# One decoder block on one Trainium2 core: the expert gather by moving residual rows and transposing, its first batch in a written TensorE order, and another order of the last gate sums and the final normalisation

## The chip, the cores and the metric

The kernel runs on one core of one Trainium2 chip, as one program. Its engines work from queues of their own and meet through semaphores: TensorE (PE: matmuls from SBUF into PSUM; PEld are its weight loads), VectorE (DVE), ScalarE (ACT), GpSimd (POOL) and SyncE (SP), which here issues nearly all DMAs. In a matmul one operand is loaded as weights and is called stationary, the other streams through and is called moving. The metric is the device time of an execution in microseconds, shown as the median of several; less is better.

## The reference

One hybrid decoder block on 256 tokens of width 2048, all fp32:

```
xn = rms_norm(x, g_mix);  z = xn @ w_in                       # 7168 columns
o  = [ HGRN2 heads (gated linear recurrence) , gated short convolution ]
x  = x + o @ w_out
hn = rms_norm(x, g_ffn)
group = top1(softmax(hn @ w_router_group))                    # 4 groups
e1,e2 = top2(softmax(logits of the 8 experts of that group))  # 32 experts
x  = x + sum over e1,e2 of  weight_e * (silu(hn@w_gate[e]) * (hn@w_up[e])) @ w_down[e]
ple = rms_norm(p @ w_ple, g_ple)
x  = x + sigmoid(x @ w_ple_gate) * ple
out = rms_norm(x, g_final)
```

All 32 experts' weights are read: 3 x 4 MB an expert.

## The kernel before

The tokens are two tiles of 128 (index j in the code); x1[j] holds the residual rows of tile j, tokens on the partitions, 2048 columns.

Weights. A list of pieces, nearly all of 1 MB, is laid down in the order of use: input projection, output projection, gate and up weights of the experts in eight batches of four, then down weights and the embedding gate's weights. `give` issues the next piece into a free slot, `take` hands out the oldest one, `refill_slot` gives a slot back and issues the next piece into it (or, while `want` is above zero, keeps the slot for another tile: three slots during the first batch, three in batch 3). A piece is thus issued once the slot's last reader is done, in the order of the list, from SP's queue.

Experts. After the routing, R1 holds for each token and expert the place of the token among that expert's 32 places. For batch b, `slot_perm` builds from it a 0/1 matrix of tokens by 4 x 32 places, scaled by the token's normalisation factor (tile Pg, lines 781 and 791). `gather(b)` returns the gathered, transposed tokens xg (16 groups of 128 columns by 128 places) and a function for a quarter of it. A quarter is eight 128x128 matmuls whose stationary operand is every fourth column of 512 of x1[j] and whose moving operand is the 0/1 matrix (line 797); VectorE multiplies the result by the gain (line 800):

```
MM(ps[:, kk], x1[j][:, kq * 512 + kk:(kq + 1) * 512:4], Pr[j], start=kk == 0 and j == 0, stop=kk == 3 and j == 1)
```

`product(b, ...)` (line 856) then makes gk and uk, 64 matmuls each in four quarters: a quarter takes four pieces, one for each expert of the batch, and each matmul writes the 32 PSUM partitions of its expert, four experts side by side. A slot is given back after its last matmul of the quarter. `hidden` makes silu(gk)·uk and transposes it (line 869). In the first batch the quarters of the gather are called between the quarters of gk; for the later ones the whole `gather(b + 1)` is called between gk and uk of batch b. `embed` (lines 881, 901) prepares the embedding beside batch 4 and 5, `weights_w` (lines 806 to 831) the routing weights beside the first product.

Down products. The first four batches are done at full width (lines 1050, 1039), the last four in five column chunks (lines 1177, 1161), each followed by the embedding gate of the chunk before: `residual` adds the chunk to x1 and transposes it (lines 1084 to 1096), `gate_mm` multiplies it with the split weights (lines 1118 to 1120) into the sums G. For the last chunk `gate_sum` puts the sum so far into a PSUM bank by a matmul with the identity (line 1128) and the gate's matmuls add to it. Eight such groups (two tiles by four times 512 columns) end the kernel: `gate` takes sigmoid and multiplies by ple, `update` adds to x1 and squares (line 1221), `mean_square`, `token_scale` and `store` are the final normalisation (lines 1234, 1235).

Order. The code is recorded and a scheduler orders each engine's instructions by priority and readiness under its own costs; `tc.issue_after(i)` forces what is recorded in it behind instruction i, and `seq()` uses it with TensorE's last instruction in state["pe"], so that a stretch of TensorE's order is the order of the code. PSUM tiles come from two pools of four banks, `bank` and `misc`; `tmp4` tiles rotate over three buffers.

Of the kernel before, what the change touches and what calls it, by code (L numbers as in the profile page):

```python
# [11 lines left out]
AF = mybir.ActivationFunctionType  # L12
OP = mybir.AluOpType
# [22 lines left out]
def kernel(ctx, tc, a, out, dbg=None):  # L36
# [24 lines left out]
    def misc(shape=(P, 512), name="ms"):  # L61
        return psB.tile(list(shape), F32, tag="ms", name=nm(name))
# [716 lines left out]
    def slot_perm(Pm, b, j):  # L779

        V.tensor_tensor(Pm[:, j], R1[:, j, 4 * b:4 * b + 4].unsqueeze(2).to_broadcast([P, 4, CAP]),
                        iota1.unsqueeze(1).to_broadcast([P, 4, CAP]), OP.is_equal)

    def gather(b):

        xg = slot(xg_slots[b % 2], [P, KT, P], name="xg")
        Pm = tmp4([P, 2, 4, CAP], "Pg")
        Pr = [Pm[:, j].rearrange("p e c -> p (e c)") for j in range(2)]
        for j in range(2):
            slot_perm(Pm, b, j)  # L790
            V.tensor_scalar(Pr[j], Pr[j], r1[:, j:j + 1], None, OP.mult)  # L791

        def quarter(kq):
            ps = misc((P, 4, P), "xg")
            for j in range(2):
                for kk in range(4):
                    MM(ps[:, kk], x1[j][:, kq * 512 + kk:(kq + 1) * 512:4], Pr[j], start=kk == 0 and j == 0,  # L797
                       stop=kk == 3 and j == 1)
            ks = slice(4 * kq, 4 * kq + 4)
            state["xg"] = V.tensor_tensor(xg[:, ks], ps, gfq[:, kq].unsqueeze(2).to_broadcast([P, 4, P]), OP.mult)  # L800
        return xg, quarter

# [43 lines left out]
    def product(b, xg, name, before=None):  # L846
        bk = bank(name=name)
        for kp in range(4):
            if before is not None:
                before(kp)  # L850
            four = [take() for _ in range(4)]
            for kk in range(4):
                k = 4 * kp + kk
                for e in range(4):
                    q = slice(32 * e, 32 * e + 32)
                    MM(bk[q], xg[:, k, q], four[e][1][:, kk], start=k == 0, stop=k == KT - 1)  # L856
            for e in range(4):
                refill_slot(four[e][0])
            step()
        return bk  # L860
# [60 lines left out]
    xg_slots = [8, None]  # L921
    xg, quarter = gather(0)

    quarter(0)
    first_xg = state["xg"]

    def first_quarters(kp):
        if kp > 0:
            quarter(kp)

    for b in range(NB):
# [18 lines left out]
        if b + 1 < NB:  # L950
            xn, quarter = gather(b + 1)
            for kq in range(4):
                quarter(kq)
        uk = product(b, xg, "uk")
# [112 lines left out]

    def seq():

        return tc.issue_after(state["pe"].ins) if "pe" in state else ExitStack()  # L1070

# [78 lines left out]

    job = None
    for ci, (c0, w) in enumerate(CHUNKS):
        last = ci == len(CHUNKS) - 1
# [12 lines left out]
        for b in range(NBR, NB):  # L1166
# [31 lines left out]
            if last and b >= NB - 2:  # L1198
                if b == NB - 2:
                    parts = {}  # L1200
                    for n in range(3):
                        gate_sum(0, n, bank)
                n = 2 * (b - NB + 2)
                for q in range(n, n + 2):
                    parts[q] = split_gate(q, [own[q // 2]], free)
        combine(*late)
        if not last:
            job = embedding_gate(c0, w, acc, ci == 0)


    xT = residual(c0, w, acc)
    with tc.issue_after(state["x2T"].ins):
        gate_sum(0, 3, misc)
        gate_sum(1, 0, misc)
    ssf = st("ssf", (2, 4))
# [10 lines left out]

    def token_scale(j):
        rsqrt_cols(rf[:, j:j + 1], msf[:, j:j + 1], 1, "rft")

    def store(j):  # L1230
        for n in range(4):
            ns = slice(n * 512, (n + 1) * 512)
            g = Gs[j][:, ns]
            V.scalar_tensor_tensor(g, x1[j][:, ns], rf[:, j:j + 1], gfin[:, ns], OP.mult, OP.mult)  # L1234
            nc.sync.dma_start(out[0, j * P:(j + 1) * P, ns], g)

    def gate(j, n):
        if (j, n) not in gb:
            with tc.issue_after(state["gate"].ins):
                gate_sum(j, n, misc)  # L1240
        gate_mm(gb[j, n], xT, parts[n], j, False)
        ns = slice(n * 512, (n + 1) * 512)
        g = Gs[j][:, ns]
        state["sig"] = A.activation(g, gb[j, n], AF.Sigmoid)
        V.tensor_tensor(g, g, ple[j][:, ns], OP.mult)

    def update(j, n):
        ns = slice(n * 512, (n + 1) * 512)
        g = Gs[j][:, ns]
        V.tensor_tensor(x1[j][:, ns], g, x1[j][:, ns], OP.add)  # L1250
        square(j, n)

    for n in range(4):
        gate(0, n)
        update(0, n)
    for n in range(4):
        gate(1, n)
        if n == 1:
            mean_square(0)
    with tc.issue_after(state["sig"].ins):  # L1260
        A.activation(warm, epsc, AF.Sqrt)
        update(1, 0)
        token_scale(0)
        update(1, 1)
        update(1, 2)
        update(1, 3)
        store(0)
        mean_square(1)
        token_scale(1)
        store(1)  # L1270

# [42 lines left out]
```

## Time and profile before

| what | value |
|---|---|
| median of 3 runs | 1502.43 us (1502.09 to 1502.65) |
| the profiled execution | 1500.68 us, span 1499.0 us |
| TensorE busy | 1333.2 us, 89% of the span |
| TensorE weight loads | 811.9 us, 54% |
| VectorE, ScalarE, GpSimd busy | 466.1, 341.1, 21.9 us |
| DMA | 505.62 MB, 337 GB/s on average |
| gate, up and down weights | 128 pieces each, 1024.0 KB a piece |
| mean granted TensorE clock | 0.965 of 2.4 GHz |

The profile is one execution on the chip. A record of TensorE is one pass: an fp32 matmul leaves two records, a transpose one. The time of a record includes the tail in which the next one already runs, so a run of records is read from start to start. The DMA share is the mean busy share of the 16 DMA engines and passes 1.0 a little where they are full. The name on the left of an arrow is what an instruction writes; a bracket at the end of a row is the idle time before it and what ended it.

### The profile page before, as it was taken

To read this page: it belongs to the slowest core of one execution; us is meant where nothing else is said; L and a number is where in the kernel's file an instruction comes from. 1 tells how busy PE (TensorE), PEld (TensorE's weight loads), DVE (VectorE), ACT (ScalarE), POOL (GpSimd) and SP (SyncE) were. 2 spreads that over 40 slices of the span, in tenths; PEclk is the share of its full clock that TensorE was granted. 3 is DMA by queue.
4 is the path that set the end of the run, shared out by engine and by line. 5 is a ranking of instruction groups with operands and counts; after the bars stand their busy time and mean duration, and the time that the engine had idled before them with its cause. 6 is when DMAs were issued, how large, how long until landed. Compare 5 with 4: busy or idle time off the path is not lost. (4 is left out here: it accounts for less than half of the span.)

```text
span 1499.0 us, 19727 instructions
## 1 busy us (share of the span) xinstructions
PE 1333.2 (89%) x8490; PEld 811.9 (54%) x8490; DVE 466.1 (31%) x750; ACT 341.1 (23%) x469; POOL 21.9 (1%) x36
## 2 busy tenths in 40 slices
PE   9999999999999986869698787866689999898995
PEld 9998999999897642415152333311122222253663
DVE  6778756575543100001011221100001111213455
ACT  6666455354441000000001000000010000222233
POOL 1001100000000000000000000000000000000000
PEclk9999999999999999989999998988999999999998
DMA  8855625479546999999999999999999999999991
GB/s 308 267 163 182 214 97 197 157 250 339 209 163 267 402 421 422 421 421 420 421 421 422 421 378 422 420 421 422 421 420 422 421 420 388 392 390 391 366 336 57
DMA packets 140377, 505.62 MB, mean 337 GB/s; under 512 B 12361, under 2 KB 33210, under 8 KB 98814
## 3 DMA queue, kind: packets, MB, share of 16 engines
q1 hardware_dynamic: 139726, 501.74, 85.9%
q0 software_dynamic: 384, 2.36, 0.4%
q8 instruction: 68, 1.11, 0.3%
q10 hardware_dynamic: 176, 0.22, 0.1%
q14 instruction: 23, 0.19, 0.0%
HBM read 502.19 MB, written 2.10 MB: 336 GB/s over the span
## 5 line engine op out<-in xcount | busy, mean ns | idle before, releaser
L856 PE MATMUL uk<-w,xg 128*32 128x512 f32 x1024 | 197.1, 687 | 92.8 <-DMA w<-in_w_up_dram 92.8
L337 PE MATMUL mm<-xh,whl 128*128 128x256 f32 x768 | 218.8, 285 | 0.3 <-ACT xh L259 0.3
L339 PE MATMUL mm<-xh,whl 128*128 128x256 f32 x768 | 217.6, 283 | 0.1
L338 PE MATMUL mm<-xl,whl 128*128 128x256 f32 x768 | 217.3, 283 | 0.3 <-DVE xl L260 0.2
L301 DVE TENSOR_TENSOR whl<-w,whl 128x1024 fp32r<-128x1024 f32 (+1 forms) x146 | 175.8, 1212 | 109.9 <-ACT whl L300 109.6
L300 ACT CAST whl<-w 128x1024 fp32r<-128x1024 f32 (+1 forms) x146 | 150.5, 1036 | 187.4 <-PE mm L339 112.1
L856 PE MATMUL gk<-w,xg 128*32 128x512 f32 x1024 | 165.7, 640 | 23.4 <-DMA w<-in_w_gate_dram 23.4
L856 PEld LDWEIGHTS uk<-w,xg 128*32 128x32 f32 x1024 | 43.3, 122 | 240.4 <-DMA w<-in_w_up_dram 165.9
L338 PEld LDWEIGHTS mm<-xl,whl 128*128 128x128 f32 x768 | 147.3, 192 | 0.9 <-DVE xl L260 0.8
L337 PEld LDWEIGHTS mm<-xh,whl 128*128 128x128 f32 x768 | 147.1, 192 | 1.1 <-ACT xh L259 0.5
L339 PEld LDWEIGHTS mm<-xh,whl 128*128 128x128 f32 x768 | 147.2, 192 | 0.4 <-DVE whl L301 0.3
L1050 PE MATMUL y<-w,hT 128*32 128x512 f32 x512 | 134.6, 603 | 6.5 <-PEq L1019 6.5
L797 PEld LDWEIGHTS xg<-Pg,x 128*128 128x128 f32 x512 | 121.4, 328 | 16.6 <-issue 15.4
L865 DVE TENSOR_TENSOR sg<-sg,uk 128x512 f32<-128x512 f32 x8 | 5.5, 688 | 389.1 <-PE uk L856 389.1
L797 PE MATMUL xg<-Pg,x 128*128 128x128 f32 x512 | 125.4, 401 | 0.7 <-DVE Pg L791 0.7
L856 PEld LDWEIGHTS gk<-w,xg 128*32 128x32 f32 x1024 | 38.6, 116 | 123.0 <-issue 73.7
L1050 PEld LDWEIGHTS y<-w,hT 128*32 128x32 f32 x512 | 37.9, 111 | 100.9 <-issue 96.9
L1177 PE MATMUL y<-w,hT 128*32 128x512 f32 (+1 forms) x640 | 77.0, 534 | 15.0 <-DMA w<-in_w_down_dram 15.0
L870 ACT COPY hT<-hT 128x256 f32<-128x256 f32 x8 | 3.0, 372 | 301.9 <-PE hT L869 301.9
L1040 DVE TENSOR_TENSOR x<-acc,x 128x512 f32<-128x512 f32 x32 | 22.1, 692 | 138.0 <-PE acc L1039 138.0
L800 DVE TENSOR_TENSOR xg<-xg,gfq 128x512 f32<-128x512 f32 x32 | 22.1, 692 | 126.3 <-PE xg L797 126.3
L1177 PEld LDWEIGHTS y<-w,hT 128*32 128x32 f32 x640 | 21.3, 112 | 64.2 <-issue 30.5
(293 smaller groups left out, 1340.2 us busy)
## 6 DMA issues: line engine op xcount, KB each, us to landing
w<-in_w_gate_dram SPq DMA_DIRECT2D x128, 1024.0 KB, 19.8
w<-in_w_up_dram SPq DMA_DIRECT2D x128, 1024.0 KB, 19.8
w<-in_w_down_dram SPq DMA_DIRECT2D x128, 1024.0 KB, 16.5
w<-in_w_in_dram SPq DMA_DIRECT2D x55, 1024.0 KB, 5.3
w<-in_w_out_dram SPq DMA_DIRECT2D x16, 1024.0 KB, 6.7
w<-in_w_ple_gate_dram SPq DMA_DIRECT2D x16, 1024.0 KB, 12.6
xa<-in_x_dram SPq DMA_DIRECT2D x8, 256.0 KB, 4.8
x<-in_x_dram POOLq DMA_DIRECT2D x2, 1024.0 KB, 8.1
```

Source lines behind the costliest of these rows:

```text
L300: state["copy"] = A.copy(wh, wf)
L301: V.tensor_tensor(wl, wf, f32(wh), OP.subtract)
L337: MM(o, wh[:, kk, cs], b_h, start=first, stop=False)
L338: MM(o, wh[:, kk, cs], b_l, start=False, stop=False)
L339: MM(o, wl[:, kk, cs], b_h, start=False, stop=last)
L797: MM(ps[:, kk], x1[j][:, kq * 512 + kk:(kq + 1) * 512:4], Pr[j], start=kk == 0 and j == 0, stop=kk == 3 and j == 1)
L800: state["xg"] = V.tensor_tensor(xg[:, ks], ps, gfq[:, kq].unsqueeze(2).to_broadcast([P, 4, P]), OP.mult)
L856: MM(bk[q], xg[:, k, q], four[e][1][:, kk], start=k == 0, stop=k == KT - 1)
L865: V.tensor_tensor(sg, sg, uk, OP.mult)
L1040: V.tensor_tensor(x1[j][:, ns], acc, x1[j][:, ns], OP.add)
L1050: MM(ys[n][q], hT[k // 2][:, k % 2, b, q], four[e][1][:, n * 512:(n + 1) * 512], start=k == 0, stop=k == 3)
L1177: last_y = MM(ys[q, :w], hT[f // 2][:, f % 2, b, q], held[e][1][:, f], start=f == 0, stop=f == 3)
```

## The change

The gather is done in two steps. `rows(kq, j)` multiplies with the 0/1 matrix as the stationary operand and 512 columns of x1[j] as the moving one, both tiles into one PSUM bank; ScalarE copies the gathered rows to SBUF. `turn(kq)` transposes every fourth column of them, four transposes a quarter, and VectorE multiplies by the gain as before. In the first batch these calls are put in TensorE's order by `seq`, the steps of the next quarters ahead of each product quarter. In the last chunk three gate sums stay where they were, one more is recorded before the last accumulation, one before `residual` and two behind it, so that one of eight is left among the groups. The squares come right behind the residual add of their group, and the two final scale chains are mixed with the output products.

```
+    def seq():
+
+        return tc.issue_after(state["pe"].ins) if "pe" in state else ExitStack()
...
-        def quarter(kq):
+        gts, pss = [], []
+
+        def rows(kq, j):
+
+            if j == 0:
+                pss.append(misc(name="xr"))
+            state["pe"] = MM(pss[kq], Pr[j], x1[j][:, kq * 512:(kq + 1) * 512], start=j == 0, stop=j == 1)
+            if j == 1:
+                if kq % 2 == 0:
+                    gts.append(tmp4([P, 2, 512], "gt"))
+                A.copy(gts[-1][:, kq % 2], pss[kq])
+
+        def turn(kq):
+
             ps = misc((P, 4, P), "xg")
-            for j in range(2):
-                for kk in range(4):
-                    MM(ps[:, kk], x1[j][:, kq * 512 + kk:(kq + 1) * 512:4], Pr[j], start=kk == 0 and j == 0,
-                       stop=kk == 3 and j == 1)
+            for kk in range(4):
+                state["pe"] = nc.tensor.transpose(ps[:, kk], gts[kq // 2][:, kq % 2, kk::4], ident)
             ks = slice(4 * kq, 4 * kq + 4)
             state["xg"] = V.tensor_tensor(xg[:, ks], ps, gfq[:, kq].unsqueeze(2).to_broadcast([P, 4, P]), OP.mult)
-        return xg, quarter
+        return xg, rows, turn
...
+            with seq() if before is not None else ExitStack():
+                for kk in range(4):
...
-    xg, quarter = gather(0)
-
-    quarter(0)
+    xg, rows, turn = gather(0)
+
+    def first(*steps):
+        for f, *args in steps:
+            with seq():
+                f(*args)
+
+    rows(0, 0)
+    first((rows, 0, 1), (rows, 1, 0), (turn, 0), (rows, 1, 1))
     first_xg = state["xg"]
 
     def first_quarters(kp):
         if kp > 0:
-            quarter(kp)
+            first((turn, kp))
+        if 0 < kp < 3:
+            first((rows, kp + 1, 0), (rows, kp + 1, 1))
...
-            xn, quarter = gather(b + 1)
+            xn, rows, turn = gather(b + 1)
             for kq in range(4):
-                quarter(kq)
+                rows(kq, 0)
+                rows(kq, 1)
+                turn(kq)
...
             if last and b >= NB - 2:
-                if b == NB - 2:
-                    parts = {}
-                    for n in range(3):
-                        gate_sum(0, n, bank)
                 n = 2 * (b - NB + 2)
                 for q in range(n, n + 2):
                     parts[q] = split_gate(q, [own[q // 2]], free)
+                if b == NB - 2:
+                    for n in range(3):
+                        gate_sum(0, n, bank)
+                else:
+                    gate_sum(0, 3, misc)
...
+    gate_sum(1, 0, misc)
     xT = residual(c0, w, acc)
-    with tc.issue_after(state["x2T"].ins):
-        gate_sum(0, 3, misc)
-        gate_sum(1, 0, misc)
+    gate_sum(1, 1, bank)
+    gate_sum(1, 2, misc)
...
     for n in range(4):
         gate(0, n)
-        update(0, n)
+    mean_square(0)
     for n in range(4):
         gate(1, n)
-        if n == 1:
-            mean_square(0)
     with tc.issue_after(state["sig"].ins):
-        A.activation(warm, epsc, AF.Sqrt)
-        update(1, 0)
-        token_scale(0)
-        update(1, 1)
-        update(1, 2)
-        update(1, 3)
-        store(0)
-        mean_square(1)
-        token_scale(1)
-        store(1)
+        rsqrt_cols(rf[:, 0:1], msf[:, 0:1], 1, "rft")
+    store(0, 0)
+    store(0, 1)
+    mean_square(1)
+    with tc.issue_after(state["sig"].ins):
+        rsqrt_cols(rf[:, 1:2], msf[:, 1:2], 1, "rft")
+    store(0, 2)
+    store(0, 3)
+    for n in range(4):
+        store(1, n)
```

**The first batch.** TensorE from the last routing instruction (cntT) to the second quarter of gk, before; xg is the gathered tile or its PSUM bank, x_327 and x_328 are x1[0] and x1[1], gk's other matmuls are left out:

```order
L768 MATMUL cntT_4942<-consts,cnt_4940 1x128
L797 MATMUL xg_4969<-Pg_4964,x_327_4098 128x128 x4
L797 MATMUL xg_4969<-Pg_4964,x_328_4100 128x128 x4
L797 MATMUL xg_4998<-Pg_4964,x_327_4098 128x128 x4
L856 MATMUL gk_4979<-w_4210,xg_4963 32x512
...
L797 MATMUL xg_4998<-Pg_4964,x_328_4100 128x128 x4
L797 MATMUL xg_5032<-Pg_4964,x_327_4098 128x128 x4
L856 MATMUL gk_4979<-w_4338,xg_4963 32x512
```

The same stretch of TensorE after; xr are the gathered rows in PSUM, gt their copy in SBUF:

```order
L768 MATMUL cntT_4942<-consts,cnt_4940 1x128
L803 MATMUL xr_4969<-x_327_4098,Pg_4964 128x512
L803 MATMUL xr_4969<-x_328_4100,Pg_4964 128x512
L803 MATMUL xr_4974<-x_327_4098,Pg_4964 128x512
L813 MATMUL xg_4976<-consts,gt_4972 128x128 x4
L803 MATMUL xr_4974<-x_328_4100,Pg_4964 128x512
L872 MATMUL gk_4984<-w_4210,xg_4963 32x512
...
L813 MATMUL xg_5003<-consts,gt_4972 128x128 x4
L803 MATMUL xr_5009<-x_327_4098,Pg_4964 128x512
L803 MATMUL xr_5009<-x_328_4100,Pg_4964 128x512
L872 MATMUL gk_4984<-w_4338,xg_4963 32x512
```

Ahead of each product quarter 12 or 8 gather matmuls of 128 columns have become row matmuls of 512 columns and four transposes, with the rows of the next quarter ahead of the product.

ScalarE at the same place before, from the table load of the square root (L179) to the routing weights (eg, ee):

```order
L179 ACT_TABLE_LOAD
L179 ACTIVATE r1t_4893<-ms_428_4889 128x2
L812 ACT_TABLE_LOAD
L812 ACTIVATE eg_5100<-eg_5100,r_429_4890 128x4
L813 ACTIVATE ee_5102<-ee_5102,r_429_4890 128x8
```

And after:

```order
L179 ACT_TABLE_LOAD
L179 ACTIVATE r1t_4893<-ms_428_4889 128x2
L807 COPY gt_4972<-xr_4969 128x512
L807 COPY gt_4972<-xr_4974 128x512
L827 ACT_TABLE_LOAD
L827 ACTIVATE eg_5102<-eg_5102,r_429_4890 128x4
L828 ACTIVATE ee_5104<-ee_5104,r_429_4890 128x8
```

The two copies of gathered rows now stand between the square root and the exponential's table load.

**Batch 5.** TensorE between the first and the second quarter of gk, where gb is a row broadcast of `embed`, before:

```order
L856 MATMUL gk_6319<-w_6263,xg_6129 32x512
L797 MATMUL xg_6479<-Pg_6464,x_327_4098 128x128 x3
L797 MATMUL xg_6479<-Pg_6464,x_328_4100 128x128 x4
L797 MATMUL xg_6489<-Pg_6464,x_327_4098 128x128 x3
L856 MATMUL gk_6319<-w_6265,xg_6129 32x512
L797 MATMUL xg_6489<-Pg_6464,x_327_4098 128x128
L797 MATMUL xg_6489<-Pg_6464,x_328_4100 128x128 x4
L797 MATMUL xg_6499<-Pg_6464,x_327_4098 128x128 x4
L797 MATMUL xg_6499<-Pg_6464,x_328_4100 128x128 x4
L881 MATMUL gb_6539<-dg_6534,consts 128x512
L856 MATMUL gk_6319<-w_6267,xg_6129 32x512
L881 MATMUL gb_6572<-dg_6567,consts 128x512
```

And after, where the main run of the second quarter begins with the last row:

```order
L803 MATMUL xr_6492<-x_327_4098,Pg_6476 128x512
L803 MATMUL xr_6492<-x_328_4100,Pg_6476 128x512
L872 MATMUL gk_6331<-w_6277,xg_6139 32x512
L813 MATMUL xg_6496<-consts,gt_6484 128x128 x4
L803 MATMUL xr_6502<-x_327_4098,Pg_6476 128x512
L803 MATMUL xr_6502<-x_328_4100,Pg_6476 128x512
L872 MATMUL gk_6331<-w_6279,xg_6139 32x512
L813 MATMUL xg_6507<-consts,gt_6505 128x128 x4
L803 MATMUL xr_6513<-x_327_4098,Pg_6476 128x512
L803 MATMUL xr_6513<-x_328_4100,Pg_6476 128x512
L813 MATMUL xg_6517<-consts,gt_6505 128x128 x2
L872 MATMUL gk_6331<-w_6281,xg_6139 32x512
```

The gather stands between the same products as before, and the two broadcasts that stood ahead of the second quarter's main run are behind it.

**The last chunk.** TensorE from the last two accumulations (acc) to the first matmul of the first group (Gf), before:

```order
L1161 MATMUL acc_8910<-y_9042,PwT_6128 128x256 x2
L1161 MATMUL acc_8910<-y_9091,PwT_6128 128x256 x2
L1092 MATMUL x2T_9106<-consts,x_327_4098 128x128
L1092 MATMUL x2T_9106<-consts,x_328_4100 128x128
...
L1128 MATMUL Gf_9113<-G_7976,consts 128x512
L1128 MATMUL Gf_9115<-G_7977,consts 128x512
L1118 MATMUL Gf_9062<-ghl_9068,x2T_9105 128x512
```

And after:

```order
L1187 MATMUL acc_8926<-y_9058,PwT_6138 128x256 x2
L1153 MATMUL Gf_9117<-G_7992,consts 128x512
L1187 MATMUL acc_8926<-y_9107,PwT_6138 128x256 x2
L1153 MATMUL Gf_9121<-G_7993,consts 128x512
L1117 MATMUL x2T_9126<-consts,x_327_4098 128x128
L1117 MATMUL x2T_9126<-consts,x_328_4100 128x128
...
L1153 MATMUL Gf_9133<-G_7993,consts 128x512
L1153 MATMUL Gf_9135<-G_7993,consts 128x512
L1143 MATMUL Gf_9084<-ghl_9078,x2T_9125 128x512
```

Two gate sums now stand ahead of the transposes, two others behind them; of the three that stood among the groups one is left.

ScalarE over the last groups before, sigmoids (L1244) and squares (L1221, junk):

```order
L1244 ACTIVATE G_7977<-Gf_9184 128x512
L1244 ACTIVATE G_7977<-Gf_9194 128x512
L1261 ACT_TABLE_LOAD
L1261 ACTIVATE warm<-epsc 128x1
L1221 ACTIVATE junk_9206,ssf_9117<-x_328_4100 128x512
L179 ACTIVATE rft_9208<-msf_9119 128x1
```

And after:

```order
L1268 ACTIVATE G_7993<-Gf_9135 128x512
L1248 ACTIVATE junk_9206,ssf_9137<-x_328_4100 128x512
L1248 ACTIVATE junk_9217,ssf_9137<-x_328_4100 128x512
L1268 ACTIVATE G_7993<-Gf_9219 128x512
L179 ACT_TABLE_LOAD
L179 ACTIVATE rft_9232<-msf_9139 128x1
L1248 ACTIVATE junk_9230,ssf_9137<-x_328_4100 128x512
```

Three squares of the second token tile stand ahead of the last sigmoid, where none stood.

## Rows read from the trace of the kernel before

**Rows 1.** Windows (us): PE, PEld, DVE, ACT, POOL busy (count), clock, DMA share, GB/s

```profile
466.00:482.00 16.00, 16.00 (x102) 10.49 (x102) 3.80 (x22) 2.25 (x5) 0.00 (x0) 1.00 0.26 83
482.00:510.00 28.00, 28.00 (x164) 21.08 (x167) 4.89 (x10) 0.60 (x1) 0.00 (x0) 1.00 1.01 422
510.00:514.00 4.00, 4.00 (x40) 1.17 (x36) 0.00 (x0) 0.00 (x0) 0.00 (x0) 1.00 0.66 219
514.00:870.00 356.00, 287.68 (x1506) 126.66 (x1498) 32.24 (x83) 10.33 (x19) 1.08 (x2) 0.94 1.01 421
870.00:882.00 12.00, 12.00 (x60) 4.59 (x63) 7.29 (x20) 0.93 (x2) 0.00 (x0) 1.00 0.72 283
...
1101.00:1240.00 139.00, 139.00 (x496) 41.17 (x495) 16.61 (x24) 8.21 (x15) 0.00 (x0) 1.00 1.01 420
```

**Rows 2.** Timeline of SP's DMA issues: start, length, engine, line, out<-in, count

```profile
479.86 16.91 SPq L162 DMA_DIRECT2D w<-in_w_up_dram  x11
...
858.05 0.86 SPq L162 DMA_DIRECT2D w<-in_w_gate_dram  x2
877.81 2.92 SPq L162 DMA_DIRECT2D w<-in_w_up_dram  x3
```

**Rows 3.** Timeline of TensorE, first batch

```profile
462.94 5.84 PE L797 MATMUL xg<-Pg,x 128*128 128x128 f32 x24
...
468.70 3.64 PE L856 MATMUL gk<-w,xg 128*32 128x512 f32 x32
472.28 4.00 PE L797 MATMUL xg<-Pg,x 128*128 128x128 f32 x16
476.20 3.64 PE L856 MATMUL gk<-w,xg 128*32 128x512 f32 x32
```

**Rows 4.** Timeline of TensorE, batch 5

```profile
851.12 3.30 PE L797 MATMUL xg<-Pg,x 128*128 128x128 f32 x14
...
859.03 1.04 PE L856 MATMUL gk<-w,xg 128*32 128x512 f32 x2
...
875.00 3.62 PE L856 MATMUL gk<-w,xg 128*32 128x512 f32 x26
```

**Rows 5.** The chain that ended last: start, length, what

```profile
1252.03 7.08 PE acc L1039 x16
...
1297.01 1.02 PE x2T L1092 x8
...
1465.61 1.94 PE acc L1161 x8
...
1468.05 0.33 PE x2T L1092
...
1468.93 1.72 PE Gf L1128 x4
...
1488.12 2.74 DVE G L1234 x4
```

**Rows 6.** Timeline of TensorE: the transposes of a hidden tile

```profile
522.94 0.75 PE L869 MATMUL hT<-consts,sg 128*128 128x128 f32 x4
```

**Rows 7.** ScalarE's groups: busy us, mean ns, idle before

```profile
L1058 ACT COPY y<-y 128x512 f32<-128x512 f32 x16 | 8.6, 592 | 138.4 <-PE y L1050 137.9
```

**Rows 8.** Timeline of ScalarE, first batch

```profile
456.55 0.20 ACT L179 ACTIVATE r1t<-ms 128x2 f32<-128x2 f32 x1
456.77 1.28 ACT L812 ACT_TABLE_LOAD   x1
467.74 0.30 ACT L812 ACTIVATE eg<-eg,r 128x4 f32<-128x4 f32 x1 [9.69 <-DVE eg L806]
```

**Rows 9.** Timeline of VectorE: the routing weights; the last output products

```profile
470.26 0.17 DVE L829 TENSOR_TENSOR ee<-ee,gp 128x16 f32<-128x16 f32 x1
...
1492.36 2.74 DVE L1234 SCALAR_TENSOR_TENSOR G<-x,rf,gfin 128x512 f32<-128x512 f32 x4
```

**Rows 10.** Timeline of TensorE at the lower clock

```profile
898.67 1.92 PE L856 MATMUL uk<-w,xg 128*32 128x512 f32 x2 [1.44 <-DMA w<-in_w_up_dram]
```

More of the change, by code (lines that the diff above doesn't have):

```diff
@@ L851, in product @@
             four = [take() for _ in range(4)]
[L852 to L856, printed above, removed]
+            with seq() if before is not None else ExitStack():
+                for kk in range(4):
+                    k = 4 * kp + kk
+                    for e in range(4):
+                        q = slice(32 * e, 32 * e + 32)
+                        last = MM(bk[q], xg[:, k, q], four[e][1][:, kk], start=k == 0, stop=k == KT - 1)
+            state["pe"] = last
             for e in range(4):
@@ L1066 @@
     gate_slots = []
-    def seq():
-        return tc.issue_after(state["pe"].ins) if "pe" in state else ExitStack()
+    state.pop("pe")
     def accumulator(w):
@@ L1151 @@
     job = None
+    parts = {}
     for ci, (c0, w) in enumerate(CHUNKS):
@@ L1225, in mean_square, with store @@
         V.tensor_scalar(msf[:, j:j + 1], msf[:, j:j + 1], 1.0 / D, EPS, OP.mult, OP.add)
[L1227 to L1235, printed above, removed]
+    def store(j, n):
+        ns = slice(n * 512, (n + 1) * 512)
+        g = Gs[j][:, ns]
+        V.scalar_tensor_tensor(g, x1[j][:, ns], rf[:, j:j + 1], gfin[:, ns], OP.mult, OP.mult)
+        nc.sync.dma_start(out[0, j * P:(j + 1) * P, ns], g)
     def gate(j, n):
         if (j, n) not in gb:
-            with tc.issue_after(state["gate"].ins):
-                gate_sum(j, n, misc)
-        gate_mm(gb[j, n], xT, parts[n], j, False)
+            gate_sum(j, n, misc)
+        with seq():
+            gate_mm(gb[j, n], xT, parts[n], j, False)
+        state["pe"] = state["gate"]
         ns = slice(n * 512, (n + 1) * 512)
@@ L1245, in gate @@
         V.tensor_tensor(g, g, ple[j][:, ns], OP.mult)
-    def update(j, n):
-        ns = slice(n * 512, (n + 1) * 512)
-        g = Gs[j][:, ns]
         V.tensor_tensor(x1[j][:, ns], g, x1[j][:, ns], OP.add)
```

## The prediction

> **What bounds the kernel now.** I read the windows first, then the SP queue, then TensorE around each hole, then the chain at the end. The windows [rows 1] show a data-bound kernel: from 514 to 870 us the DMA engines stand at share 1.01 and 421 GB/s while TensorE is busy 287.68 of 356 us. The reader should look for the three stretches that fall below that rate: 466 to 482 us at 83 GB/s, 510 to 514 at 219, 870 to 882 at 283. Against 421 GB/s they lose 16·(1−83/421) = 12.8, 4·(1−219/421) = 1.92 and 12·(1−283/421) = 3.93 us. What is lost there is not caught up: behind each hole the engines run at their ceiling again, and at 1101 to 1240 us TensorE (139.00 of 139.00 us) and the DMA engines (420 GB/s) are full together. That later part starts when the last gate and up weights arrive and holds nothing that is tied to absolute time, so I pass an earlier stream to the end one for one.
>
> The SP queue tells what makes the holes [rows 2]. The run of refills begins at 479.86 us; in the later hole nothing is issued between 858.05 (plus 0.86) and 877.81. A slot is free when its last product of a quarter is done, so the holes are TensorE being late. TensorE there [rows 3, 4]: in the first batch 24 records of gather from 462.94 us, a product quarter from 468.70, 16 gather records of 4.00 us from 472.28, the next quarter from 476.20, whose first freed slot gives the issue at 479.86 (3.66 later). In batch 5 the gather sits between two quarters of the product, the second of which starts its main run only at 875.00.
>
> **The gather.** A quarter of a gather costs 4.00 us now (an fp32 matmul leaves two records, a batch 64). After, it is two matmuls of 512 columns and four transposes. The trace has the first shape under another name: 16 records in 7.08 us [rows 5], 0.44 each, so the two take 4·0.44 = 1.77 us. Transposes with every fourth column as the stationary operand exist too, one record each: four are begun at 522.94 and end 0.75 later [rows 6]. Four unstrided ones take 1.02/2 = 0.51 us [rows 5]; four at the pace of today's gather records would take 1.0. I take 0.58, near the strided row without its tail. So 2.35 us a quarter (2.3 to 2.8) against 4.00. New is a ScalarE copy between the two steps, 592 ns as such copies take now [rows 7]; with some 0.25 us of drain and signalling (an estimate from the 0.16 that a 0.75 us group outlasts its pace, and the hand-over) it is 0.85 us that other TensorE work must cover.
>
> *First batch.* Rows of quarter 0: 462.94 to 464.71. The copy ends about 465.55; under it runs the first half of quarter 1's rows. Transposes to 466.2, VectorE's scaling to about 467.0, under it the second half of quarter 1. The first product starts at 467.0 instead of 468.70. Then 3.58 of product (468.70 to 472.28), 0.58 of transposes and 1.77 of rows: the second quarter starts at 472.9 instead of 476.20, and the first big refill is issued 3.3 us earlier, near 476.55. Later refills come every 5.9 us for four pieces of 1024 KB, which take 10 us to move at 421 GB/s, so the stream then holds. The cover that could go: VectorE's scaling of quarter 1 stands behind the routing weights. Now ScalarE loads the exponential's table at 456.77, long before its use at 467.74 [rows 8]; after, the two copies stand ahead of that load. Second copy done at 467.8, load 1.28, exponentials from 469.1, 1.35 us later than now; the weights, now done at 470.26+0.17 [rows 9], end at 471.8, the scaling at 472.5, still 0.4 us ahead of the product at 472.9. A further 1.28 us there, the price of one more load, would leave 0.9 uncovered: 2.4 as the lower end.
>
> In rows 8 the load stands right behind the square root (456.55 plus 0.20, then 456.77) and takes 1.28 us. The Trainium skill, page "ScalarE: Activation LUTs", section "What ACT_TABLE_LOAD costs", puts a drain of about 1380 ns beside a load of about 1283 ns, some 2.66 us a switch. The trace agrees with its load and shows no drain. By the row this place gives 3.3 us; by the rule 1.38 more stands in the chain, 1.0 of it in the open, and the place gives 2.3.
>
> *Second hole.* It comes because the whole gather for batch 1 runs before the first up quarter frees a slot. After, four pieces are refilled after each of the next three gate quarters (476.5, 482.5, 488): 12 pieces, 30 us, from about 478.5 to 508. The first up quarter has 8.5 of gather, about 1 of uncovered copies and up to 4.8 of product in front and frees its slots near 502. The hole closes: 1.9 (0 to 1.9).
>
> *Third hole.* TensorE now does 14 gather records from 851.12, the first quarter's main run, then the rest of the gather among single products (1.04 each [rows 4]) and two row broadcasts, then the second run at 875.00. After: 1.77 of rows in place of 3.30, so the first run, now over some 1.1 us before 859.03, ends near 856.4; then three and a half sets of transposes and three of rows, 3.5·0.58+3·1.77 = 7.3, three singles 3.0, one copy in the open 0.85; the broadcasts move behind. The second run starts near 867.6, not 875.00, the issue comes near 870.4, not 877.81. Data follows an issue by about 2 us (479.86 to 482), so of the 12·283/421 = 8.1 us' worth moved between 870 and 882 only about 2 came from the late issue, and the older pieces last to about 876 at the full rate. The hole closes with 3 us in hand: 3.9 (0 to 3.9; not below, since the new quarter at its upper 2.8 and the open copy stay under 4.00). In the other batches TensorE waits for data anyway, and 6.6 us less work there is worth nothing.
>
> **The end.** From the last down product on TensorE has one gap [rows 5]: the two last accumulations end at 1465.61+1.94 = 1467.55, the transposes start at 1468.05 and, with a wait between them for the second VectorE add, end at 1468.93. After, one gate sum stands between the accumulations and one behind them: the 0.5 us are filled, and the four transposes run in 0.51 instead of 0.88. The eight groups and eight sums stay as many and as long; two sums still cover the split of the transposed tile (1.72). TensorE is done 0.9 us earlier. Behind it two effects meet. ScalarE has the square of the group before last ahead of the last sigmoid; it waits for VectorE, which has a multiply and an add for each group and no slack, so the last sigmoid starts up to 0.85 us later than TensorE allows. On the other side the second scale chain, which now puts 1492.36−(1488.12+2.74) = 1.5 us between the two runs of output products [rows 5, 9], is mixed into the first run and costs about 0.5. I take them as equal: 0.9 for the end (−0.5 to 1.5).
>
> **Sum.** 3.3+1.9+3.9+0.9 = 10.0 us. The profiled execution took 1500.68 us (span 1499.0), so 1490.7 for it; the median shown, 1502.43, lies 1.75 higher, and for a median I forecast 1492.4. The bounds: 2.4+0+0−0.5 = 1.9 to 3.5+1.9+3.9+1.5 = 10.8 us less, 1500.5 to 1491.6.
>
> **Rivals.**
> *The third hole stays.* With less to do TensorE waits more for data, and its clock may fall. It is granted 0.94 in 514 to 870 us [rows 1], and one pair of product records takes 1.92 us at 898.67 [rows 10] against 1.04. At that level the 11 us of gather and singles double and the issue slips past 877. Against it: 1.00 in 870 to 882. Gain 6.1, 1496.3 us. The Trainium skill, page "TensorE: Matmul & The Clock Gate", section "HAM oscillation — how this bites in real kernels", says that a TensorE with too little work between its waits for data keeps falling back to the half clock; the 0.94 agrees in kind, and by that rule this rival is what comes.
> *The weights come late.* One more load's worth in ScalarE's part of the first batch: 0.9 us less, 1493.3.
> *Hidden after all.* If something behind the holes made up for lost time, only the end would count: 1501.5. Against it: share 1.01 from 514 to 870.
> *Slower: the first batch loses the clock.* The new order makes TensorE wait for a copy and a scaling before the first product. If the clock fell to its lower level there (1.2 in place of 2.4 GHz, records twice as long, as in rows 10), the first product would last 7.2 us, the second quarter start at 478.7 and its first refill be issued near 486, 6 us later than now, which eats what the other three places give (6.7). If it lasts into the third quarter, each further quarter (11.9 us for 10 us of data) and the up quarter with its gather (some 27 us) open new holes, the largest of 17 us: from the third quarter on it decides for slower; through the up quarter 6+2+17−6.7 = 18 us more, about 1520. Against it: 1.00 in 466 to 514 us.
>
> **How the numbers follow.** Forecast (all four places, 1491.3 to 1493.0): 0.62. Third hole stays, wholly or half: 0.15. Weights late: 0.08. Hidden: 0.06. Slower: 0.04. More than forecast: 0.05. This kernel's runs tell about 0.2% (3 us) from no change. Faster by that are 0.62+0.15+0.08+0.05 = 0.90, less 0.02 for small mishaps that add up: 0.88; within 0.06+0.02 = 0.08; slower 0.04. The range 1490.6 to 1497.0 holds the forecast, the late weights, the open third hole and a little more than the forecast.
>
> **What would show it.** Right: the run of refills begins near 476.5 us; no window below 415 GB/s between 480 and 1090; everything behind starts about 9 us earlier; 2.35 us of TensorE for a quarter of the gather; no TensorE gap from the last accumulation to the last gate matmul. Wrong: a hole that remains near 870; a first product over 4 us; four transposes near 1 us; a second quarter that waits for VectorE's scaling; a tail behind the last matmul over 1 us longer than now.

## The result and the profile after

The changed kernel takes 1492.12 us (median of four, 1491.95 to 1492.46) against 1502.54 for the kernel before in the same set (1502.09 to 1505.28): ratio 0.9927, 95% interval 0.991 to 0.9944. 10.4 us are gone; the forecast was 10.0, 1492.4 us. The profiled execution took 1492.06 us (span 1490.4), 8.6 us less than the profiled one of before, which lay 1.8 below its median.

The windows of the changed kernel, to be laid beside [rows 1]:

```profile
466.00:482.00 16.00, 16.00 (x115) 5.30 (x114) 5.05 (x26) 3.91 (x8) 0.00 (x0) 1.00 0.46 171
510.00:514.00 4.00, 3.09 (x26) 1.26 (x19) 0.78 (x2) 0.37 (x1) 0.00 (x0) 1.00 1.01 422
514.00:870.00 356.00, 279.88 (x1306) 77.41 (x1305) 34.62 (x88) 21.66 (x38) 1.07 (x2) 0.92 1.01 421
870.00:882.00 12.00, 10.38 (x73) 2.77 (x72) 5.43 (x17) 2.25 (x3) 0.00 (x0) 1.00 1.02 424
```

The last column, the rate of the stream in GB/s, is to be read first. The first stretch went from 83 to 171 GB/s and now loses 16·(1−171/421) = 9.5 us where it lost 12.8; the second and third holes are gone. At 882 us the stream is 3.3+1.9+3.9 = 9.1 us ahead. SP's issues give the same two dates [rows 2]:

```profile
476.53 2.04 SPq L162 DMA_DIRECT2D w<-in_w_up_dram  x4
...
865.86 14.18 SPq L162 DMA_DIRECT2D w<-in_w_up_dram  x10
```

The run of refills begins at 476.53 instead of 479.86, and the issue that came at 877.81 comes at 865.86. TensorE in the first batch, beside [rows 3]:

```profile
462.69 2.81 PE L803 MATMUL xr<-x,Pg 128*128 128x512 f32 x6
465.37 0.75 PE L813 MATMUL xg<-consts,gt 128*128 128x128 f32 x4
465.96 1.02 PE L803 MATMUL xr<-x,Pg 128*128 128x512 f32 x2
466.91 3.64 PE L872 MATMUL gk<-w,xg 128*32 128x512 f32 x32
470.48 0.75 PE L813 MATMUL xg<-consts,gt 128*128 128x128 f32 x4
471.07 1.88 PE L803 MATMUL xr<-x,Pg 128*128 128x512 f32 x4
472.88 3.64 PE L872 MATMUL gk<-w,xg 128*32 128x512 f32 x32
```

Four transposes step on after 0.59 us, four records of rows after 1.81: 2.40 us a quarter (forecast 2.35, before 4.00). The product quarters start at 466.91 and 472.88 (forecast 467.0 and 472.9). No row has an idle time in brackets: copy and scaling are covered. The routing weights, which could have spoilt that, on ScalarE and VectorE, beside [rows 8, 9]:

```profile
467.02 0.59 ACT L807 COPY gt<-xr 128x512 f32<-128x512 f32 x1 [1.70 <-PE xr L803]
467.62 1.28 ACT L827 ACT_TABLE_LOAD   x1
468.92 0.30 ACT L827 ACTIVATE eg<-eg,r 128x4 f32<-128x4 f32 x1
```
```profile
471.34 0.17 DVE L844 TENSOR_TENSOR ee<-ee,gp 128x16 f32<-128x16 f32 x1
471.43 0.68 DVE L815 TENSOR_TENSOR xg<-xg,gfq 128x512 f32<-128x512 f32 x1
```

The load starts 0.01 us after the copy's end and takes 1.28; weights done at 471.5 (forecast 471.8), scaling at 472.11, 0.77 us before the product wants it. The Trainium skill, "ScalarE: Activation LUTs", section "What ACT_TABLE_LOAD costs", adds a drain of some 1380 ns to a load; no row here shows one, since the load follows the copy and the first exponential follows the load (end 468.90, start 468.92) with 0.02 us or less between.

TensorE in batch 5, beside [rows 4]:

```profile
848.00 3.62 PE L872 MATMUL gk<-w,xg 128*32 128x512 f32 x26
...
862.62 0.51 PE L813 MATMUL xg<-consts,gt 128*128 128x128 f32 x2 [0.68 <-ACT gt L807]
863.05 3.62 PE L872 MATMUL gk<-w,xg 128*32 128x512 f32 x26
```

A run is the 26 records that a quarter does in one piece once its last weights are there. From first run to second it is 15.05 us instead of 20.65 (before, the first run starts at 854.35), with one copy in the open (0.68, forecast 0.85).

The end, on TensorE, ScalarE and VectorE; the first fence is the changed kernel, the second the kernel before:

```profile
1456.87 1.93 PE L1203 MATMUL y<-w,hT 128*32 128x256 f32 x32
...
1476.12 0.40 PE L1145 MATMUL Gf<-ghl,x2T 128*128 128x512 f32 x1
...
1476.51 0.63 ACT L1248 ACTIVATE junk<-x 128x512 f32<-128x512 f32 x1 [0.63 <-DVE x L1270]
1477.14 0.58 ACT L1268 ACTIVATE G<-Gf 128x512 f32<-128x512 f32 x1
...
1480.28 1.41 DVE L1257 SCALAR_TENSOR_TENSOR G<-x,rf,gfin 128x512 f32<-128x512 f32 x2
...
1483.63 2.74 DVE L1257 SCALAR_TENSOR_TENSOR G<-x,rf,gfin 128x512 f32<-128x512 f32 x4
```
```profile
1463.68 1.93 PE L1177 MATMUL y<-w,hT 128*32 128x256 f32 x32
...
1483.87 0.40 PE L1120 MATMUL Gf<-ghl,x2T 128*128 128x512 f32 x1
...
1484.30 0.60 ACT L1244 ACTIVATE G<-Gf 128x512 f32<-128x512 f32 x1 [1.66 <-PE Gf L1120]
```

Measured from the start of the last down product (its 32 records), TensorE is done 0.94 us earlier (19.25 against 20.19), the last sigmoid starts 0.35 earlier (20.27 against 20.62: the square ahead of it takes 0.6 back), and the last output products start 1.92 earlier (26.76 against 1492.36−1463.68 = 28.68, [rows 9]).

So the pair of profiles adds up: the last down product starts 1463.68−1456.87 = 6.81 earlier, the end adds 1.92, together 8.7; the two profiled times differ by 8.6. Of the 9.1 that the stream had at 882 us, 6.8 arrived. Where the other 2.3 went is taken up below.

### The profile page after: what moved, and what is told of

Its sections match the earlier page's. It is cut to its first block, busy times and chain, and to the rows that moved or that the text cites. A ratio compares the mean times of both kernels' runs of the same rounds, so it can differ in the third digit from the quotient of the medians.

```text
span 1490.4 us, 19275 instructions
## 1 busy us (share of the span) xinstructions
PE 1312.2 (88%) x8234; PEld 729.1 (49%) x8234; DVE 466.0 (31%) x750; ACT 359.8 (24%) x500; POOL 22.0 (1%) x36
## 5 line engine op out<-in xcount | busy, mean ns | idle before, releaser
L872 PE MATMUL uk<-w,xg 128*32 128x512 f32 x1024 | 203.5, 711 | 89.2 <-DMA w<-in_w_up_dram 89.2
L872 PE MATMUL gk<-w,xg 128*32 128x512 f32 x1024 | 187.0, 656 | 37.5 <-DMA w<-in_w_gate_dram 37.5
L803 PE MATMUL xr<-x,Pg 128*128 128x512 f32 x128 | 61.4, 599 | 0.7 <-DVE Pg L795 0.7
L1134 DVE TENSOR_TENSOR ghl<-w,ghl 128x1024 fp32r<-128x1024 f32 x32 | 38.9, 1222 | 48.4 <-ACT ghl L1133 48.1
```

What stands on the lines that cost most here:

```text
L803: state["pe"] = MM(pss[kq], Pr[j], x1[j][:, kq * 512:(kq + 1) * 512], start=j == 0, stop=j == 1)
L872: last = MM(bk[q], xg[:, k, q], four[e][1][:, kk], start=k == 0, stop=k == KT - 1)
L1134: V.tensor_tensor(t[:, 1], src, f32(t[:, 0]), OP.subtract)
```

## The experiments

Each kernel was timed in five rounds beside the kernel before: 1503.36 us in the first set, 1503.02 in the second, 1502.19 in the third. Differences are against the changed kernel's second timing, 1491.99, which belongs to the first set. The intervals are some 2 us wide to either side: only the old gather in batch 6 lies clear of the changed kernel by them, the early refills touch it, and the other differences are carried by dates in the traces more than by the times. One caution: the step ahead of the first batch (the transpose cntT) starts at 462.45 to 464.12 us in the profiles of kernels with the same code up to there. Instants of two profiles are only comparable after that shift.

**The changed kernel once more.**

> The changed kernel once more, as the base for the three runs beside it. Theory (three holes in the weight stream closed, and a shorter end): 1492.1 us as in its first runs, no stretch below 415 GB/s between 480 and 1250 us. Side question: 9.2 us more of stream at 882 us was only 7.3 us at the last up quarter; in the first trace the quarters' arrivals slip by 1.4 us near 1030 us, in a stretch of full rate with one instruction packet. If that slip is the place of that packet in this program, it stands at the same place again; if it is chance, it is elsewhere or gone.

1491.99 us, 0.9932 (0.9919 to 0.9945). The third hole came back in part:

```profile
862.00:874.00 12.00, 11.32 (x48) 3.49 (x46) 4.98 (x13) 0.92 (x2) 0.00 (x0) 1.00 0.99 388
874.00:882.00 8.00, 7.28 (x61) 2.42 (x64) 4.62 (x16) 1.66 (x2) 0.00 (x0) 1.00 0.96 395
```

12·(1−388/421)+8·(1−395/421) = 1.4 us, because batch 5 began 3.1 us later. What delayed it is TensorE's clock in the up quarter just ahead of batch 5. The first profile of the changed kernel, then this one:

```profile
833.10 3.19 PE L872 MATMUL uk<-w,xg 128*32 128x512 f32 x25 [1.43 <-DMA w<-in_w_up_dram]
833.00:841.00 8.00, 7.06 (x39) 2.60 (x40) 1.51 (x3) 0.96 (x2) 0.00 (x0) 1.00 1.02 424
```
```profile
833.28 6.15 PE L872 MATMUL uk<-w,xg 128*32 128x512 f32 x25 [1.43 <-DMA w<-in_w_up_dram]
833.00:841.00 8.00, 6.87 (x31) 1.64 (x32) 0.69 (x1) 0.00 (x0) 0.00 (x0) 0.61 1.01 419
```

The same 25 records start 0.18 us apart and take 3.19 us at a granted clock of 1.00 and 6.15 at 0.61, behind single products with waits for data of 1.3 to 1.5 us between them. So the lower level cost 3.0 us here, about what the prediction had in hand, and 1.4 of it came back as a hole. The execution was no slower for it (1491.27 us). The kernel with the late square, below, has the same: 6.01 us for these records at 0.57, and 404 and 407 GB/s in the two windows, 0.8 us lost. The slip near 1030 us, told of at the end, is here 0.7 instead of 1.4.

**The old gather in one batch**, in batch 0, in batch 1 (ahead of the first up quarter), in batch 6 (done during batch 5):

```diff
+                if b + 1 in (6,):          # (1,) in the second; batch 0: quarter(0), quarter(kp)
+                    quarter(kq)
+                    continue
                 rows(kq, 0)
                 rows(kq, 1)
                 turn(kq)
```

> The changed kernel with the old gather (16 fp32 products a quarter) in batch 0 alone. Theory, the first batch is worth what its first refill moves: second gate quarter starts at 476.2 instead of 472.9 us, first big refill is issued near 479.8 instead of 476.3, everything behind 3.3 us later: 1495.4 us. Rival, the gain of the first batch is not kept (the stream meets something else later): within 0.5 us of the changed kernel, 1492.1 to 1492.6, and the start of the down stage no later than 1086.1 us.

> The changed kernel with the old gather in batch 1 alone, the one that stands before the first up quarter. Theory, it made the hole at 510 to 514 us: with the refills now begun 3.3 us earlier and this gather 6.5 us longer, the pieces run out near 508 us before the up quarter frees the next: a hole of 2 to 4 us at half the rate, 1.9 to 3 us lost: 1494.0 to 1495.1 us. Rival, the second hole was closed by the first batch's earlier end and not by the shorter gather of batch 1: no window below 415 GB/s from 500 to 520 us, 1492.1 us.

> The changed kernel with the old gather in batch 6 alone, the one done during batch 5 among row broadcasts. Theory, it made the hole at 870 us: the second run of the gate product starts 6.6 us later than now (863.0), near 869.7, the next issue comes near 872.5 instead of 865.9, and the pieces in flight end near 873: a hole of 1.5 to 3.9 us of lost data at 870 to 882 less 9: 1493.6 to 1496.0 us. Rival, the hole closed because the stream runs 5 us earlier against the table of other work there: full rate at 860 to 880 us, 1492.1 us.

Batch 0: 1494.74 us, 2.75 more: 0.9949 (0.9937 to 0.9961); its window 466 to 482 is back at 81 GB/s. Right, a little under 3.3; its six times (1493.99 to 1497.38) all lie above the five of the changed kernel (1491.27 to 1493.83). Batch 1: 1492.35, 0.4 more, no difference that can be told: 0.9932 (0.9919 to 0.9945). The rival holds, since 510 to 514 us stays full. It does so too with the old gather in batch 0 (second row):

```profile
510.00:514.00 4.00, 4.00 (x44) 1.24 (x40) 0.00 (x0) 0.00 (x0) 0.00 (x0) 1.00 1.02 424
510.00:514.00 4.00, 4.00 (x40) 1.17 (x36) 0.00 (x0) 0.00 (x0) 0.00 (x0) 1.00 1.00 416
```

With the long gather of batch 1 the first up quarter starts at 503.04 us, 39.3 behind cntT (463.72), against 45.3 before (508.04, cntT 462.71): the first batch's shorter quarters alone bring it forward by 6.0. Batch 6: 1496.66, 4.67 more: 0.9962 (0.9949 to 0.9975), above its forecast:

```profile
862.00:874.00 12.00, 12.00 (x55) 7.55 (x58) 4.91 (x11) 0.00 (x0) 0.00 (x0) 1.00 0.74 310
874.00:882.00 8.00, 8.00 (x56) 2.15 (x52) 3.80 (x14) 1.66 (x2) 0.00 (x0) 1.00 0.75 292
```

This hole loses 3.2+2.5 = 5.6 us, more than the 3.9 of before. The issue that ends it comes at 874.88, 9.0 later than in the changed kernel's first profile, since that execution's batch 5 also began 2.0 late: the 25 records ahead of it took 4.89 us at a granted clock of 0.79 (833 to 841 us), 1.7 more than at the full level. The profiled execution took 1498.05 us, 1.4 above its median, so the 4.67 and the 5.6 do not contradict each other.

**The old end.** The last part of the function, from the loop over the chunks on, is that of the kernel before:

```diff
-    gate_sum(1, 0, misc)
     xT = residual(c0, w, acc)
-    gate_sum(1, 1, bank)
-    gate_sum(1, 2, misc)
+    with tc.issue_after(state["x2T"].ins):
+        gate_sum(0, 3, misc)
+        gate_sum(1, 0, misc)
...
```

> The changed kernel with the end of the kernel before. Theory by the two profiles (TensorE done 0.95 us earlier, the last sigmoid 0.6 us late by the square ahead of it, 1.45 us less between that sigmoid and the last store): 1.8 us slower than the changed kernel, 1493.8 us. Forecast of the prediction for this part: 0.9 us, 1492.9. Rival, the two effects behind TensorE cancel or the end is hidden: 1492.0 to 1492.3. Beside it, on the stream: no hole at 870 us, so the arrivals of weight pieces slip by 0.8 to 1.5 us between 1015 and 1035 us, as in three kernels without that hole; in the two kernels with it they did not.

1494.21 us (1492.48 to 1494.41), 2.2 more: 0.994 (0.9926 to 0.9953). In its profile the last products start 28.68 us after the last down product, to the hundredth as before. By these dates the end is worth 1.9 us, twice the forecast.

**The first batch in plain order.**

```diff
-    first((rows, 0, 1), (rows, 1, 0), (turn, 0), (rows, 1, 1))
+    first((rows, 0, 1), (turn, 0))
...
-            first((turn, kp))
-        if 0 < kp < 3:
-            first((rows, kp + 1, 0), (rows, kp + 1, 1))
+            first((rows, kp, 0), (rows, kp, 1), (turn, kp))
```

> The changed kernel with the first batch in plain order: rows, copy, transposes and scaling of a quarter right before its product, nothing of the next quarter between. Theory, the order covers the copy (0.85 us) and the scaling (1.0): the first product starts as now (near 467.0), the second at 474.7 instead of 472.9, the first big refill 1.8 us later, 1493.5 us (the old first batch, 3.3 us later, cost 2.75). Rival, the waits cost TensorE its clock: records at twice the length in the first batch, second quarter after 478 us, 1496 us or more. Other rival, order does not matter: 1492.0.

1493.36 us, 1.4 more: 0.9938 (0.9925 to 0.9952). TensorE's timeline:

```profile
464.12 0.27 PE L768 MATMUL cntT<-consts,cnt 128*1 128x128 f32 x1
...
468.57 3.64 PE L872 MATMUL gk<-w,xg 128*32 128x512 f32 x32 [0.78 <-DVE xg L815]
...
476.59 3.62 PE L872 MATMUL gk<-w,xg 128*32 128x512 f32 x32
```

The first product comes 4.45 us after cntT, as in the changed kernel (4.46). The second comes after 12.47 instead of 10.43: 2.0 us for the uncovered copy and scaling (forecast 1.8). The waits did not cost the clock: granted 1.00 from 466 to 514 us. So the written order moves the second product by 2.0 us; the 1.4 us in the time agree with that but lie within the intervals. The slower rival does not come even with the waits in the open.

**More work in the last up product's waits.** An extra product stands behind each of the first three matmuls of a quarter, and the quarter's matmuls are held in their order:

```diff
+                        if extra and kk == 0 and e > 0:
+                            with tc.issue_after(last.ins):
+                                last = MM(junk, ident, x1[0][:, 0:512], start=True, stop=True)
```

> The changed kernel with twelve extra 128x512 products (results not used) in TensorE's waits for data in the last up product, one after each single of a quarter. Theory, the last quarter at the lower clock (5.28 us for 26 records instead of 3.62) gives away 1.7 us of what the stream won: now 3.62 in every run, the down stage starts at 1085.0 or before, and the time is 0.5 to 0.9 us lower, 1491.2 us (the two profiles of the changed kernel differ in the same way, 1490.4 and 1489.5 us of span). Rival, what follows is bound by the stream and takes no notice: 1492.0. Other rival, the extra work delays the products: later than 1086.1 us there, and slower.

1491.47 us (1490.95 to 1494.39), 0.9926 (0.9913 to 0.994): 0.5 less, inside what can be told. The two profiles of the changed kernel, then this one, at the last up quarter:

```profile
1073.13 5.28 PE L872 MATMUL uk<-w,xg 128*32 128x512 f32 x26 [1.32 <-DMA w<-in_w_up_dram]
```
```profile
1073.38 3.62 PE L872 MATMUL uk<-w,xg 128*32 128x512 f32 x26 [1.34 <-DMA w<-in_w_up_dram]
```
```profile
1074.27 3.62 PE L877 MATMUL uk<-w,xg 128*32 128x512 f32 x26 [0.28 <-DMA w<-in_w_up_dram]
```

The same kernel runs that quarter at the full level (second profile, granted 1.00 from 1073 to 1080 us) or in part at half of it (first profile, 0.76). In the first profile this gave away 1.66 us. With the waits filled it ran at the full level, but its last down product starts 994.1 us after cntT, between the other two (994.4 and 993.4). Whether the lower level there costs anything at the end stays open; the bound is about 1 us. The Trainium skill, "TensorE: Matmul & The Clock Gate", section "HAM oscillation — how this bites in real kernels", expects such falls in a TensorE that waits for data. The rows agree, here (0.76) and in the up quarter ahead of batch 5 (0.61); whether an execution has the fall at a given quarter differs from one to the next.

**The square behind the last sigmoid.**

```diff
-        square(j, n)
+        if (j, n) != (1, 2):
+            square(j, n)
...
     with tc.issue_after(state["sig"].ins):
+        square(1, 2)
         rsqrt_cols(rf[:, 0:1], msf[:, 0:1], 1, "rft")
```

> The changed kernel with the square of the group before last behind the last sigmoid instead of ahead of it. Theory, the square (waiting for VectorE's add) holds the last sigmoid 0.6 us behind the last gate product: now the sigmoid starts within 0.05 us of that product's end, the scale chain 0.6 us earlier, and the end 0.3 to 0.6 us: 1491.5 us. Rival, the output products on VectorE have the second scale chain as their limit, which the later square moves back: 1492.0 or more.

1491.6 us, 0.9923 (0.9909 to 0.9937): no difference that can be told. The sigmoid starts at 1476.37 behind a product that ends at 1476.34, as expected, but the last products start 26.55 us after the last down product instead of 26.76. Of 0.6 us 0.2 is left; the second scale chain is then the limit, as the rival said.

**The first refills earlier.** Three slots freed by the first gate quarter are set aside (for the next xg and hT), so one refill goes out at 470.6 us and the run starts at 476.5. Here they are taken from the third quarter: first in the changed kernel, then with the late square, then in the kernel before.

```diff
-        if b == 0:
-            want[0] += 3
...
     def first_quarters(kp):
+        if kp == 2:
+            want[0] += 3
```

> The changed kernel, with the three slots that are set aside for other tiles taken from the third gate quarter of the first batch instead of the first: the first quarter's four slots are then all refilled at once, near 470.6 us, where now one is (a lone piece moves at 472 to 474.5 us and the stream begins at 478). Theory, the stream's start is worth itself: full rate from 472.3 us, the window 466 to 482 us loses 6.0 us instead of 9.5, everything behind up to 3.5 us earlier, and by the share that came through for the old first batch (2.75 of 3.3) 2.9 us: 1489.1 us. Rival, the same number of pieces stands ready before the first up quarter gives slots back, so the stream runs dry near 504.5 us instead: a hole there of 2 us or more, 1490.5 to 1492.0.

> The two together: early refill, and the square of the group before last behind the last sigmoid (which shortened the end by 0.2 us in its own profile: last products 26.55 instead of 26.76 us behind the start of the last down product). Theory 0.2 us below the early refill alone, 1488.9 us; rival, no difference that can be told.

> The kernel before, with the same three slots taken from the third gate quarter. Theory, its first refill comes near 472.4 us, but with the old gather of batch 1 (13.3 us of records in one run) the first up quarter still starts at 508 and gives slots back near 511.7: 13 pieces from 474.3 us last to 506.6, and the hole that was 510 to 514 becomes 7 us long; of 3.5 us won at the start 1.5 or less remains, 1501.0 to 1502.5. Rival, the win is independent of the gather: 1499.5 us or less.

In the changed kernel 1488.27 us (1487.94 to 1488.81): 0.9904 (0.9889 to 0.9919), 3.7 us below the changed kernel's 1491.99. The two were timed in different sets; by the ratios to the kernel before the gain is 0.9932−0.9904, some 4 us, with intervals that just touch, and the trace agrees: the last down product starts 989.5 us after cntT, 4.9 and 3.9 before those of the changed kernel's two profiles. The forecast, 2.9 us and no new hole, is right in kind and a little low. With the square 1487.83: 0.9906 (0.989 to 0.9921), no difference to tell. In the kernel before 1503.05 against 1502.19: 1.0005 (0.9996 to 1.0014), no difference, and a little above its forecast (1501.0 to 1502.5). The same edit in the two kernels, changed first:

```profile
474.00:478.00 4.00, 4.00 (x35) 0.96 (x33) 0.64 (x4) 0.58 (x1) 0.00 (x0) 1.00 1.00 418
...
508.00:514.00 6.00, 5.33 (x52) 1.43 (x44) 0.50 (x1) 0.00 (x0) 0.00 (x0) 1.00 1.01 421
```
```profile
474.00:478.00 4.00, 4.00 (x28) 2.98 (x31) 0.69 (x1) 0.00 (x0) 0.00 (x0) 1.00 0.90 360
...
508.00:514.00 6.00, 6.00 (x55) 2.09 (x58) 0.69 (x1) 0.00 (x0) 0.00 (x0) 1.00 0.16 26
```

Both fill 474 to 478 us (the changed kernel without the edit has 88 GB/s there). With the old gather the pieces then run out before the first up quarter, and 6·(1−26/421) = 5.6 us are lost. This version beats both kernels.

## Why the prediction was right, step by step

- *What bounds the kernel: the weight stream, in three holes.* Shown. Old gathers put back in batch 0 and batch 6 cost 2.75 and 4.67 us, and filling more of the first hole gives some 3.7 more. The second hole's 1.9 has no price of its own (next but one).
- *First batch, 3.3.* The start of the refills moved by 3.33, 3.07 of it measured from cntT; the price put back is 2.75.
- *Second hole, 1.9, by the shorter gather of batch 1.* The hole closed, but the reason was incomplete. Either the shorter first batch (424 GB/s with the old gather in batch 1) or the shorter gather (416 with the old one in batch 0) closes it alone, so undoing the second costs 0.4, which is no difference. The step failed in looking at batch 1 without what the first batch moves: from that alone the up quarter comes 6.0 us earlier and the stream's start only 3.1, and the 2.9 between them is more than the hole's 1.9.
- *Third hole, 3.9, with 3 us in hand.* Closed in the first profile. From the row broadcast ahead of it (850.18 us before, 845.26 after) the second run comes 7.0 us sooner, forecast 7.4. The margin was too large and taken as fixed: with batch 5 3.0 us later 1.4 us were lost again, with it 2.6 later (late square) 0.8, so some 1.6 to 1.8 us were in hand (an estimate from these two, if every microsecond beyond the margin is lost). What used it up was the lower clock in the quarter ahead.
- *The end, 0.9.* Mis-sized: 1.92 in the profile, 2.2 in the time. TensorE's part (0.94) and the late sigmoid (0.6) were right. The step that failed is taking the shorter way behind the sigmoid as equal to the delay ahead of it: it is (28.68−20.62)−(26.76−20.27) = 1.57 us against 0.6. Of it 0.9 is the second scale chain mixed into the first products (forecast 1.0), and 0.7 was left out: the first output product comes 1480.28−1477.14 = 3.14 behind the last sigmoid instead of 1488.12−1484.30 = 3.82, since a warming square root and a square, which ScalarE did between its table load and the first scale chain (1486.21 to 1486.93 us before), no longer stand there.
- *An earlier stream passes to the end one for one.* Too simple. In the two profiles 9.1 at 882 us became 1080.42−1073.13 = 7.3 at the last up quarter and 6.8 at the last down product. Of the first 1.8 lost, 1.4 is the slip told of at the end; the last up quarter then ran 1.66 longer at the lower level in the changed kernel's profile, of which no more than 0.5 shows. The over-estimate here (2.3) and the under-estimate at the end (1.0), with the 1.8 by which the profiled execution of before lay below its median, make up the close sum: that the total came within 0.4 us is in part luck.
- *Rivals.* Half clock: in the first batch and in batch 5 itself the granted clock was 1.00. But the rival of the third hole came true in part, one quarter earlier than it was looked for: in two of the ten profiles with the new gather there the fall ahead of batch 5 opened the hole by 1.4 and 0.8 us, of its 3.9. Late weights: 0.77 us to spare. Hidden after all: excluded by the old gathers.

The four undone singly (2.75, 0.36, 4.67, 2.22) add up to 10.0 us. That the sum fits is partly luck: each carries the spread of the times, the second and the first are not independent, and the third is partly the clock.

## What to carry to other kernels

In a kernel bound by one stream, look for the windows in which the stream falls below its rate, and price a change by the date at which the engine that frees buffers issues the next refill. Two fixes of the same gap do not add, and a fix at the head of a stream is worth nothing while a later gap eats it: early refills gave nothing in the old kernel and some 3.7 us in the new. Align two profiles on a common instruction before reading differences of a microsecond. Look at a second profile before trusting a margin of a few microseconds, and at the granted clock in the stretch ahead of the place as well as in it.

## What was not expected

A weight piece can arrive late while the stream is at its full rate. TensorE's timeline of the changed kernel, single products that start as pieces land:

```profile
1019.50 1.04 PE L872 MATMUL gk<-w,xg 128*32 128x512 f32 x2 [1.45 <-DMA w<-in_w_gate_dram]
1022.00 6.02 PE L872 MATMUL gk<-w,xg 128*32 128x512 f32 x30 [1.45 <-DMA w<-in_w_gate_dram]
1030.88 1.05 PE L872 MATMUL gk<-w,xg 128*32 128x512 f32 x2 [2.86 <-DMA w<-in_w_gate_dram]
```

Elsewhere such a main run and the next single are 7.46 us apart (1012.04 to 1019.50); here it is 8.88, with 419 GB/s from 1022 to 1034 us, and the 1.4 us are not made up before the last up quarter. Eight profiles without a hole at 870 us have a slip of 0.8 to 1.5 us between 990 and 1040; the three with the full hole (before, old gather in batch 6, early refill in before) have none. Of the two with a part of the hole one slips by 0.7 (the changed kernel's second), the other not at all (late square). So in these profiles the closing of the hole mostly goes with a later loss of a fifth to two fifths of its 3.9 us; that the one causes the other is not shown. The cause is open: an instruction packet of 1.0 us on a DMA engine lies in that stretch (1028 us), but the old gather in batch 6 has one at 1026 and the late square one at 1030, both without a slip, so the packet alone does not explain it.
